# Hybrid attention layer on one core: probabilities transposed through HBM and VectorE instead of TensorE, x loaded a second time for the residual

## The chip, the cores and the metric

One core of a Trainium2 chip runs the whole program. Its engines are TensorE (PE in the profile; PEld is its weight load), VectorE (DVE), ScalarE (ACT), GpSimd (POOL) and SyncE (SP). Each takes its instructions in the order in which they were written for it and waits at an instruction until what it needs is there. Transfers are issued from the queues of SP, ACT and POOL. The metric is the device time of one execution in microseconds, as the median of several runs.

## The reference

One decoder layer on x (256 tokens x 2048), float32. Two groups of eight heads share one input projection: A, a dilated sliding-window attention with three window/dilation pairs, and B, a latent attention with low-rank q and kv. Each head's probabilities are a softmax over the keys that a query may see, and they multiply V. Then comes the output projection, a residual with RMSNorm, and a feed-forward part with squared ReLU.

```python
h = _rmsnorm(x, norm_attn_pre)
a_q, a_k, a_v, c_q, c_kv, k_r = split(h @ w_in)
# A: rotary on 32 of 128 channels, windows (128,1), (512,4), (2048,16), merged by softmax denominators
# B: q = rms(c_q) @ w_uq, [k | v] = rms(c_kv) @ w_ukv, one rotary key shared by the heads
s = einsum('bqhd,bkhd->bhqk', q, k) * scale;  s = where(key <= query, s, -1e30)
o = einsum('bhqk,bkhd->bqhd', softmax(s), v)
x = x + _rmsnorm(concat(A, B) @ w_out, norm_attn_post)
u = square(relu(_rmsnorm(x, norm_mlp_pre) @ w_up))
x = x + _rmsnorm(u @ w_down, norm_mlp_post)
```

## The kernel before

Tokens stand in two blocks of 128 (b = 0, 1), in an order in which 32x32 blocks and a rearranged trip through HBM give a full transpose: token 32 q + t of a block stands at place 4 t + q. Weights arrive as float32 tiles of 128 x 1024 on SP's queue (`raw`, five buffers), and each is split into a high part by ScalarE and a low part by VectorE (`hi`, `lo`, eight buffers each, lines 310 to 319); a product is then three TensorE passes (hi hi, hi lo, lo hi) of 512 columns. `Weights.get` keeps the splitting six tiles ahead of TensorE's place.

The order of all work is written out by a planner, `Flow` (lines 135 to 173). It has a clock that only TensorE's products move (0.2158 for one of 512 columns), and chains, which are Python generators: each emits some instructions and then yields the time after which its next part is due. `pump`, called after each group of products, lets the due chains emit. So the delays in the tables `DA`, `DB`, `D_PAIR` and others settle where in each engine's row an instruction stands; `flow.finish` and `flow.until` run chains until a condition holds, whatever their delays.

The stages: x @ w_in for A in two halves of four heads, ([q|k], v) and (q, k, v); then c_kv with the rotary key, then c_q; B's projections k0, qr, q0, v0, k1, q1, v1 (four heads in each); the output projection; and the feed-forward part, which takes two thirds of the time.

- `prelude` (lines 564 to 580) loads x by rows, in eight pieces of 256 KB into two tiles `x0`, `x1` that stay in SBUF until the residual, and afterwards squares them on ScalarE. Their sum gives `rstd_pre` (a power on GpSimd), by which the evacuations of q, k and v scale. `tables` (582 to 604) makes the rotary table `trig` on VectorE and by a Sin on ScalarE.
- `evac_a` (673 to 700): q and k of A leave PSUM on ScalarE, are rotated on VectorE, and are transposed per head: written to HBM on GpSimd's queue with rearranged rows, loaded back, and turned in 32x32 blocks by VectorE (line 698).
- `softmax_pv` (620 to 655), for every head: VectorE adds the mask and takes the maximum (626), ScalarE takes exponentials with their sums (637), VectorE normalizes (640, 642), TensorE transposes the three 128x128 blocks of probabilities that are not masked out into a PSUM bank (646), ScalarE copies them to `pT` (648), TensorE multiplies with V (653, 654), and `split` writes the head's rows of `mixT`.
- `heads_a` and `heads_b` (658 to 671, 827 to 843) run heads as workers of the planner: two workers with two heads each for a half of A, three workers for B's eight heads. Scores `sc` and outputs `o` take the PSUM banks 6 and 7 in turn (`at_bank`).
- `powers` and `residual` (895 to 952) scale x by a power of two and add the normalized output projection to it. `out_evac` uses the gains `g_post`, loaded on SP when the first block of the output projection is done (line 977), together with the release of the attention's pool `pb`.

## Time and profile before

| | us |
|---|---|
| median of 3 runs | 1031.03 (1030.07 to 1031.07) |
| profiled execution | 1030.5 |
| its span, first to last instruction | 1028.7 |
| TensorE busy | 1017.2 |
| VectorE busy | 832.2 |
| ScalarE busy | 631.3 |
| GpSimd busy | 73.4 |

The granted clock of TensorE was 0.998 over the span. In rows of the profile, a group stands as: line, engine, operation, out<-in, shapes, count, then its busy time in us and the mean ns of one, then the idle time before it and what ended it. In a timeline a row begins with the start and the length in us. Products overlap in TensorE's pipeline, so the distance between starts, not the length of one, is what a product costs its queue. The 256 tokens' attention lies between about 65 and 290 us; the output projection ends at about 343 us.

### The profile page before, as it was taken

To read this page: it belongs to the slowest core of one execution; us is meant where nothing else is said; L and a number is where in the kernel's file an instruction comes from. 1 tells how busy PE (TensorE), PEld (TensorE's weight loads), DVE (VectorE), ACT (ScalarE), POOL (GpSimd) and SP (SyncE) were. 2 spreads that over 40 slices of the span, in tenths; PEclk is the share of its full clock that TensorE was granted. 3 is DMA by queue.
4 is the path that set the end of the run, shared out by engine and by line. 5 is a ranking of instruction groups with operands and counts; after the bars stand their busy time and mean duration, and the time that the engine had idled before them with its cause. 6 is when DMAs were issued, how large, how long until landed. Compare 5 with 4: busy or idle time off the path is not lost.

```text
span 1028.7 us, 13299 instructions
## 1 busy us (share of the span) xinstructions
PE 1017.2 (99%) x4726; PEld 848.3 (82%) x4726; DVE 832.2 (81%) x1109; ACT 631.3 (61%) x838; POOL 73.4 (7%) x116
## 2 busy tenths in 40 slices
PE   9999999999999999999999999999999999999996
PEld 6888889888888888888888888888888888888885
DVE  6677647574656669998989999898999999899796
ACT  6575536565545567666775767566666665757571
POOL 0020000000001000000000100000110000211100
PEclk9999999999999999999999999999999999999999
DMA  9978457552466387777989878679979877888972
GB/s 294 361 251 268 154 179 239 177 177 84 144 225 204 104 336 259 266 255 244 297 256 303 269 243 275 195 263 340 351 268 378 287 251 255 301 313 300 317 253 82
DMA packets 106035, 257.65 MB, mean 250 GB/s; under 512 B 8944, under 2 KB 27888, under 8 KB 105584
## 3 DMA queue, kind: packets, MB, share of 16 engines
q1 hardware_dynamic: 65200, 175.14, 50.9%
q0 software_dynamic: 17392, 61.87, 18.0%
q10 hardware_dynamic: 23376, 19.78, 6.1%
q8 instruction: 37, 0.61, 0.2%
q14 instruction: 30, 0.25, 0.1%
HBM read 226.88 MB, written 29.89 MB: 250 GB/s over the span
## 4 chain that ended last, share of the span: by engine, by line
PE 85%; DMA 6%; DVE 4%; ACT 2%; issue 2%; POOL 0%; SPq 0%; DVEq 0%; POOLq 0%; ACTq 0%
PE acc_u L303 26%; PE y L303 23%; PE acc_o L303 8%; PE m L303 6%; PE md L303 5%; DMA raw<-in_w_in 4%; PE acc_k L303 3%; PE acc_v L303 3%; PE acc_ckv L303 2%; PE acc_cq L303 2%; PE acc_q L303 2%; DVE lo L314 2%; DMA ab_down<-in_w_down 1%; ACT hi L313 1%; PE sc_b L303 1%
## 5 line engine op out<-in xcount | busy, mean ns | idle before, releaser
L314 DVE TENSOR_TENSOR lo<-raw,hi 128x1024 fp32r<-128x1024 f32 (+2 forms) x205 | 232.8, 1158 | 82.8 <-ACT hi L313 81.5
L313 ACT ACTIVATE hi<-raw 128x1024 fp32r<-128x1024 f32 (+2 forms) x205 | 202.2, 1005 | 80.9 <-DMA raw<-in_w_in 23.0
L303 PE MATMUL acc_u<-hi,hT_lo 128*128 128x512 f32 x386 | 150.5, 390 | 0.4 <-DVE hT_lo L314 0.4
L303 PE MATMUL acc_u<-hi,hT_hi 128*128 128x512 f32 x386 | 150.9, 391 | 0.0
L303 PE MATMUL acc_u<-lo,hT_hi 128*128 128x512 f32 x386 | 150.3, 389 | 0.0
L303 PE MATMUL y<-lo,uhi 128*128 128x512 f32 x358 | 139.6, 390 | 0.2
L303 PE MATMUL y<-hi,uhi 128*128 128x512 f32 x358 | 139.4, 389 | 0.0
L303 PE MATMUL y<-hi,ulo 128*128 128x512 f32 x358 | 139.4, 389 | 0.0
L317 ACT ACTIVATE hi<-raw,gcol 128x1024 fp32r<-128x1024 f32 x86 | 97.1, 1149 | 36.3 <-DMA raw<-in_w_up 15.8
L318 DVE SCALAR_TENSOR_TENSOR lo<-raw,gcol,hi 128x1024 fp32r<-128x1024 f32 x86 | 106.9, 1275 | 9.6 <-ACT hi L317 9.3
L303 PEld LDWEIGHTS acc_u<-hi,hT_lo 128*128 128x128 f32 x386 | 72.5, 188 | 15.8 <-DVE hT_lo L314 0.8
L303 PEld LDWEIGHTS acc_u<-lo,hT_hi 128*128 128x128 f32 x386 | 72.5, 188 | 14.9
L303 PEld LDWEIGHTS acc_u<-hi,hT_hi 128*128 128x128 f32 x386 | 72.5, 188 | 14.9
L303 PEld LDWEIGHTS y<-lo,uhi 128*128 128x128 f32 x358 | 67.2, 188 | 14.9 <-DVE lo L314 1.1
L303 PEld LDWEIGHTS y<-hi,ulo 128*128 128x128 f32 x358 | 67.2, 188 | 14.0
L303 PEld LDWEIGHTS y<-hi,uhi 128*128 128x128 f32 x358 | 67.2, 188 | 13.9
L314 DVE TENSOR_TENSOR lo<-st_down,hi 128x1024 fp32r<-128x1024 f32 x46 | 55.0, 1219 | 0.6 <-ACT hi L313 0.6
L313 ACT ACTIVATE hi<-u 128x1024 fp32r<-128x1024 f32 (+1 forms) x33 | 32.2, 979 | 30.2 <-PE y L303 11.5
L303 PE MATMUL acc_o<-hi,mixT_hi 128*128 128x512 f32 x128 | 50.5, 395 | 0.0
L313 ACT ACTIVATE hi<-st_down 128x1024 fp32r<-128x1024 f32 x46 | 47.7, 1048 | 3.9 <-DVE st_down L370 2.5
L303 PE MATMUL md<-hi,s 128*128 128x512 f32 x138 | 50.0, 389 | 0.0
L303 PE MATMUL acc_o<-hi,mixT_lo 128*128 128x512 f32 x128 | 49.9, 390 | 0.0
(348 smaller groups left out, 2029.8 us busy)
## 6 DMA issues: line engine op xcount, KB each, us to landing
raw<-in_w_up SPq DMA_DIRECT2D x86, 512.0 KB, 4.8
raw<-in_w_down SPq DMA_DIRECT2D x82, 512.0 KB, 6.1
raw<-in_w_in SPq DMA_DIRECT2D x55, 512.0 KB, 5.3
ab<-in_w_up POOLq DMA_DIRECT2D x17, 1024.0 KB, 7.0
raw<-in_w_out SPq DMA_DIRECT2D x32, 512.0 KB, 4.8
ab_down<-in_w_down POOLq DMA_DIRECT2D x11, 1024.0 KB, 8.9
ulo<-ukeep POOLq DMA_DIRECT2D x20, 512.0 KB, 6.4
rkeep<-r ACTq DMA_DIRECT2D x28, 256.0 KB, 3.5
```

The costliest lines, as they stand in the source:

```text
L303: nc.tensor.matmul(out, a, b, start=start, stop=stop)
L313: nc.scalar.activation(hi, src, AF.Copy)
L314: nc.vector.tensor_tensor(out=lo, in0=src, in1=hi.bitcast(F32), op=OP.subtract)
L317: nc.scalar.activation(hi, src, AF.Copy, scale=g)
L318: nc.vector.scalar_tensor_tensor(out=lo, in0=src, scalar=g, in1=hi.bitcast(F32), op0=OP.mult, op1=OP.subtract)
```

## The change

The probabilities are no longer transposed on TensorE. ScalarE writes the exponentials straight into `pT`, with the columns of the three blocks rearranged, and VectorE normalizes them there. GpSimd's queue writes `pT` to HBM in runs of 96 numbers with rearranged rows (`keep`), and loads it back into `s`; VectorE turns `s` in 32x32 blocks into `pT`. V's product and the split follow as before, the split with its columns put back in order. The three PSUM transposes and the ScalarE copy of each head are gone. The planner's delays for the new steps are `D_TRIP`. A's halves have four workers with one head each, B has six, with as many buffers of `s`, `pT` and `st`.

To make room, x is not kept: `prelude` loads it in four halves of 512 KB into the buffers that q and k of A's second half use later (two of them, so that the third half waits for the first half's square), and squares each half as it comes. Two new loads of 1 MB, behind that of `g_post` on SP, bring x back for the residual. Two pads change their size, which keeps the places of the tiles in memory.

```diff
--- before.py
+++ after.py
@@ -82,7 +82,8 @@
 
 N_WARM = 8
 B_ORDER = ("k0", "qr", "q0", "v0", "k1", "q1", "v1")
-N_WORK = 3
+N_WORK = (4, 6)
+D_TRIP = (1.0, 6.0, 8.0)
 OUT_PIECES = ((0, 0, 512), (1, 0, 512), (2, 0, 512), (3, 0, 256), (3, 256, 256))
 
 
...
@@ -552,7 +553,7 @@
     weights.after[0] = [x_first]
     weights.emit(2)
 
-    xs = [mix.tile([P, D], F32, name=f"x{b}") for b in range(NB)]
+    xs = []
     cst = mix.tile([P, 704], F32, name="cst")
     freq, bias_a, bias_b = cst[:, 0:192], cst[:, 192:448], cst[:, 448:704]
     pos_i = con.tile([P, NB], I32, name="pos_i")
@@ -561,21 +562,28 @@
     ss0h = con.tile([P, NB, 2], F32, name="ss0h")
     rstd0 = []
 
+    squared = []
+
+    def square_of(half, b, pc):
+        junk = pa.tile([P, 1024], BF16, tag="v", name=f"junk0_{b}{pc}")
+        nc.scalar.activation(junk, half, AF.Square, accum_out=ss0h[:, b, pc:pc + 1])
+        squared.append((b, pc))
+        yield 0
+
     def prelude():
         yield D_X0
         nc.scalar.dma_start(out=gcol, in_=io["gains"])
-        for pc in range(4):
-            for b in range(NB):
-                c = slice(pc * 512, (pc + 1) * 512)
-                nc.sync.dma_start(out=xs[b][:, c], in_=io["x"][b * P:(b + 1) * P, c])
-                yield D_X
-        yield D_SS
         for b in range(NB):
             for pc in range(2):
-                c = slice(pc * 1024, (pc + 1) * 1024)
-                junk = pa.tile([P, 1024], BF16, tag="v", name=f"junk0_{b}{pc}")
-                nc.scalar.activation(junk, xs[b][:, c], AF.Square, accum_out=ss0h[:, b, pc:pc + 1])
-                yield 1.5
+                half = pa.tile([P, NB + 1, 512], F32, tag="qk"[pc], name=f"xh{b}{pc}")
+                half = half.rearrange("p b n -> p (b n)")[:, :1024]
+                for i in range(2):
+                    c = slice(i * 512, (i + 1) * 512)
+                    nc.sync.dma_start(out=half[:, c], in_=io["x"][b * P:(b + 1) * P, pc * 1024 + i * 512:][:, :512])
+                    yield D_X
+                flow.start(square_of(half, b, pc), D_SS)
+        while len(squared) < 4:
+            yield 1.0
         nc.vector.reduce_sum(ss0, ss0h, axis=mybir.AxisListType.X)
         rstd0.append(rstd_of(ss0, NB, D, "pre"))
 
@@ -587,8 +595,8 @@
         yield D_TAB[1]
         pos_f = con.tile([P, NB], F32, name="pos_f")
         nc.vector.tensor_copy(pos_f, pos_i)
-        ang = pa.tile([P, 2, NB, 96], F32, tag="s", bufs=2, name="ang")
-        kk_ = pa.tile([P, 2, NB, 96], F32, tag="s", bufs=2, name="kk_")
+        ang = pa.tile([P, 2, NB, 96], F32, tag="s", bufs=N_WORK[0], name="ang")
+        kk_ = pa.tile([P, 2, NB, 96], F32, tag="s", bufs=N_WORK[0], name="kk_")
         for w in range(2):
             for b in range(NB):
                 nc.vector.tensor_scalar_mul(ang[:, w, b, :], freq[:, w * 96:(w + 1) * 96], pos_f[:, b:b + 1])
@@ -619,12 +627,16 @@
 
     def softmax_pv(wk, dl, sc, bias, scale, v, head, name, need=lambda: True):
 
-        s = wk.tile([P, 384], F32, tag="s", bufs=2 if wk is pa else N_WORK, name=f"s_{name}")
-        st = wk.tile([P, 8], F32, tag="st", bufs=3, name=f"st_{name}")
-        spans = ((0, 128, bias[:, 128:256]), (128, 384, bias))
-        for i, (a, e, m) in enumerate(spans):
+        n = N_WORK[wk is not pa]
+        s = wk.tile([P, 384], F32, tag="s", bufs=n, name=f"s_{name}")
+        pT = wk.tile([P, 384], F32, tag="pT", bufs=n, name=f"pT_{name}")
+        st = wk.tile([P, 8], F32, tag="st", bufs=n, name=f"st_{name}")
+        e = pT.rearrange("p (a k c) -> p k a c", a=4, k=3)
+        spans = ((0, 1, bias[:, 128:256]), (1, 3, bias))
+        for i, (f, l, m) in enumerate(spans):
+            c = slice(f * P, l * P)
             nc.vector.tensor_tensor_reduce(
-                out=s[:, a:e], in0=sc[:, a:e], in1=m, op0=OP.add, op1=OP.max, scale=1.0,
+                out=s[:, c], in0=sc[:, c], in1=m, op0=OP.add, op1=OP.max, scale=1.0,
                 scalar=-3e38, accum_out=st[:, i:i + 1])
         if isinstance(scale, float):
             scales = [scale] * 2
@@ -633,26 +645,30 @@
             scales = [scale[:, 0, b:b + 1] for b in range(NB)]
             nc.vector.tensor_tensor(out=st[:, 2:4], in0=st[:, 0:2], in1=scale[:, 1, :], op=OP.mult)
         yield dl[2]
-        for i, (a, e, m) in enumerate(spans):
-            nc.scalar.activation(s[:, a:e], s[:, a:e], AF.Exp, bias=st[:, 2 + i:3 + i], scale=scales[i],
-                                 accum_out=st[:, 4 + i:5 + i])
+        for i, (f, l, m) in enumerate(spans):
+            nc.scalar.activation(e[:, f:l], s[:, f * P:l * P].rearrange("p (k a c) -> p k a c", a=4, c=32),
+                                 AF.Exp, bias=st[:, 2 + i:3 + i], scale=scales[i], accum_out=st[:, 4 + i:5 + i])
         yield dl[3]
         nc.vector.reciprocal(st[:, 6:8], st[:, 4:6])
-        for i, (a, e, m) in enumerate(spans):
-            nc.vector.tensor_scalar_mul(s[:, a:e], s[:, a:e], st[:, 6 + i:7 + i])
-        yield dl[4]
-        tp = tp_bank(f"pT_{name}")
-        for c in range(3):
-            transpose(tp[:, c * P:(c + 1) * P], s[:, c * P:(c + 1) * P])
-        pT = wk.tile([P, 384], F32, tag="pT", bufs=2 if wk is pa else N_WORK, name=f"pT_{name}")
-        nc.scalar.activation(pT, tp[:, :384], AF.Copy)
+        for i, (f, l, m) in enumerate(spans):
+            nc.vector.tensor_scalar_mul(e[:, f:l], e[:, f:l], st[:, 6 + i:7 + i])
+        yield D_TRIP[0]
+        keep = dram.tile([P, 384], F32, name=f"keep_{name}")
+        nc.gpsimd.dma_start(out=keep.rearrange("(a t) (q x) -> (t q) a x", a=4, q=4),
+                            in_=pT.rearrange("m (a x) -> m a x", a=4))
+        yield D_TRIP[1]
+        nc.gpsimd.dma_start(out=s, in_=keep)
+        yield D_TRIP[2]
+        nc.vector.transpose(pT.rearrange("p (k q t) -> p k q t", k=3, q=4),
+                            s.rearrange("p (q k c) -> p k q c", q=4, k=3))
         yield dl[5]
         while not need():
             yield 0.5
         o = at_bank(f"o_{name}")
         mm(o[:, :S], v[0], pT[:, :S], True, False, 2 * MM)
         mm(o[:, P:S], v[1], pT[:, S:384], False, True, MM)
-        split(mixT[0][:, head, :], mixT[1][:, head, :], o[:, :S])
+        hi, lo = [t[:, head, :].rearrange("p (b t q) -> p b t q", b=NB, q=4) for t in mixT]
+        split(hi, lo, o[:, :S].rearrange("p (b q t) -> p b t q", b=NB, q=4))
 
 
     def heads_a(qkv, half, hs, after, delay):
@@ -718,7 +734,7 @@
                 evacs.append(flow.start(evac_a(t, [[acc[i]] for acc in accs], nm, half)))
             flow.pump()
         flow.finish(*heads)
-        heads = [flow.start(heads_a(qkv, half, hs, evacs, d), 2.0) for hs, d in (((0, 1), 2.5), ((2, 3), 2.5 + D_PAIR))]
+        heads = [flow.start(heads_a(qkv, half, (h,), evacs, 2.5 + h * D_PAIR), 2.0) for h in range(4)]
 
 
     early.release()
...
@@ -865,7 +881,7 @@
                 nc.scalar.activation(t[:, h:h + 2, :].rearrange("p h s -> p (h s)"), acc, AF.Copy)
         made.add(what)
         if what == "q0":
-            workers = [flow.start(heads_b(range(w, HB, N_WORK)), w * D_PAIR) for w in range(N_WORK)]
+            workers = [flow.start(heads_b(range(w, HB, N_WORK[1])), w * D_PAIR) for w in range(N_WORK[1])]
 
 
     ssy = [con.tile([P, 4], F32, name=f"ssy{b}") for b in range(NB)]
@@ -977,6 +993,9 @@
                 nc.sync.dma_start(out=late["g_post"],
                                   in_=io["norm_attn_post"].partition_broadcast(P).rearrange("p o d -> p (o d)"))
                 late["yg"] = [po.tile([P, D], F32, name=f"yg{b}") for b in range(NB)]
+                for b_ in range(NB):
+                    xs.append(po.tile([P, D], F32, name=f"x{b_}"))
+                    nc.sync.dma_start(out=xs[b_], in_=io["x"][b_ * P:(b_ + 1) * P, :])
                 pw_chain = flow.start(powers())
             out_evac(n, b, acc[0])
             if n == 3:
```

In the changed file the lines up to 555 are numbered one higher, and later ones up to 19 higher.

**ScalarE's row in the opening.** Before; `hi23` to `hi26` are the high parts of weight tiles, `junk0` the squares of x, `ss0h` their sums:

```order
L313 ACTIVATE hi23_533<-raw23_531 128x1024
L577 ACTIVATE junk0_00_540,ss0h_127<-x0_121 128x1024
L604 ACT_TABLE_LOAD
L604 ACTIVATE trig_125<-ang_477 128x384
L577 ACTIVATE junk0_01_552,ss0h_127<-x0_121 128x1024
L313 ACTIVATE hi24_556<-raw24_554 128x1024
L577 ACTIVATE junk0_10_569,ss0h_127<-x1_122 128x1024
L313 ACTIVATE hi25_576<-raw25_574 128x1024
L577 ACTIVATE junk0_11_586,ss0h_127<-x1_122 128x1024
L313 ACTIVATE hi26_596<-raw26_594 128x1024
L680 ACTIVATE q_0_527<-acc_qk0_0_0_0_128,rstd_pre_605 128x512
L680 ACTIVATE q_0_527<-acc_qk0_0_1_0_130,rstd_pre_605 128x512
```

With the change:

```order
L314 ACTIVATE hi20_464<-raw20_462 128x1024
L569 ACTIVATE junk0_10_475,ss0h_125<-xh10_383 128x1024
L314 ACTIVATE hi21_495<-raw21_493 128x1024
L314 ACTIVATE hi22_519<-raw22_517 128x1024
L314 ACTIVATE hi23_541<-raw23_539 128x1024
L569 ACTIVATE junk0_11_548,ss0h_125<-xh11_442 128x1024
L696 ACTIVATE q_0_535<-acc_qk0_0_0_0_126,rstd_pre_555 128x512
L696 ACTIVATE q_0_535<-acc_qk0_0_1_0_128,rstd_pre_555 128x512
L696 ACTIVATE k_0_536<-acc_qk0_0_0_1_127,rstd_pre_555 128x512
L696 ACTIVATE k_0_536<-acc_qk0_0_1_1_129,rstd_pre_555 128x512
L612 ACT_TABLE_LOAD
L612 ACTIVATE trig_123<-ang_485 128x384
```

The squares have moved up, each behind the first split whose tile was loaded after that half of x; the evacuations of q and k stand ahead of the splits of tiles 24 to 26, and the table load and the Sin now stand behind the evacuations.

**GpSimd's row in A's first half.** Before, the trips of q and k of the second half:

```order
L695 DMA k_0_528<-keepk00_632 128x512
L695 DMA k_0_528<-keepk01_633 128x512
L691 DMA keepq10_911<-q_1_888 128x4x128
L691 DMA keepq11_912<-q_1_888 128x4x128
L695 DMA q_1_888<-keepq10_911 128x512
L695 DMA q_1_888<-keepq11_912 128x512
```

With the change, the heads' trips and those trips share the row (`keep_a` is a write of probabilities, `s_a` their load):

```order
L657 DMA keep_a00_870<-pT_a00_795 128x4x96
L657 DMA keep_a01_913<-pT_a01_827 128x4x96
L660 DMA s_a00_794<-keep_a00_870 128x384
L657 DMA keep_a02_947<-pT_a02_859 128x4x96
L707 DMA keepq10_955<-q_1_929 128x4x128
L707 DMA keepq11_956<-q_1_929 128x4x128
L660 DMA s_a01_826<-keep_a01_913 128x384
L657 DMA keep_a03_984<-pT_a03_896 128x4x96
L660 DMA s_a02_858<-keep_a02_947 128x384
L711 DMA q_1_929<-keepq10_955 128x512
L711 DMA q_1_929<-keepq11_956 128x512
L660 DMA s_a03_895<-keep_a03_984 128x384
```

A head's load stands behind the write of the next head or the next two; the loads of heads 1 to 3 also stand behind the writes of q, which wait for its rotation.

**TensorE's row in B.** Before, the products with V of the first three heads (`o_b`) and the scores of the next three (`sc_b`), which begin behind them; nine transposes `pT_b` stand seven places ahead of this piece:

```order
L303 MATMUL o_b0_2371<-pT_b0_2351,vB_1882 128x256
L303 MATMUL o_b0_2371<-pT_b0_2351,vB_1882 128x128
L303 MATMUL o_b1_2376<-pT_b1_2357,vB_1882 128x256
L303 MATMUL o_b1_2376<-pT_b1_2357,vB_1882 128x128
L303 MATMUL o_b2_2381<-pT_b2_2363,vB_1882 128x256
L303 MATMUL o_b2_2381<-pT_b2_2363,vB_1882 128x128
L303 MATMUL sc_b3_2386<-kT_1879,qT_1880 128x128
L303 MATMUL sc_b3_2386<-krT_1874,qrT_1881 128x128
L303 MATMUL sc_b3_2386<-kT_1879,qT_1880 128x256
L303 MATMUL sc_b3_2386<-krT_1874,qrT_1881 128x256
L303 MATMUL sc_b4_2391<-kT_1879,qT_1880 128x128
L303 MATMUL sc_b4_2391<-krT_1874,qrT_1881 128x128
```

With the change:

```order
L304 MATMUL o_b2_2523<-pT_b2_2222,vB_1876 128x256
L304 MATMUL o_b2_2523<-pT_b2_2222,vB_1876 128x128
L304 MATMUL sc_b6_2528<-kT_1873,qT_1874 128x128
L304 MATMUL sc_b6_2528<-krT_1868,qrT_1875 128x128
L304 MATMUL sc_b6_2528<-kT_1873,qT_1874 128x256
L304 MATMUL sc_b6_2528<-krT_1868,qrT_1875 128x256
L304 MATMUL o_b3_2533<-pT_b3_2247,vB_1876 128x256
L304 MATMUL o_b3_2533<-pT_b3_2247,vB_1876 128x128
L304 MATMUL sc_b7_2538<-kT_1873,qT_1874 128x128
L304 MATMUL sc_b7_2538<-krT_1868,qrT_1875 128x128
L304 MATMUL sc_b7_2538<-kT_1873,qT_1874 128x256
L304 MATMUL sc_b7_2538<-krT_1868,qrT_1875 128x256
```

With the change no transposes of probabilities are in the row, and `o_b3` stands between the scores of heads 6 and 7, which take the two banks in turn with the outputs.

4 lines of the change are left out of this document (2 added, 2 removed).

## The prediction

> **What bounds the kernel now.** I read the page's busy times first, then the table by stage, then the groups and the timeline of TensorE in the attention stages.
>
> ```profile
> span 1028.7 us, 13299 instructions
> PE 1017.2 (99%) x4726; PEld 848.3 (82%) x4726; DVE 832.2 (81%) x1109; ACT 631.3 (61%) x838; POOL 73.4 (7%) x116
> ...
> 100.00:130.00 30.00, 30.00 (x145) 25.03 (x145) 19.85 (x41) 14.30 (x27) 4.07 (x6) 1.00 0.55 170
> 220.00:250.00 30.00, 29.07 (x198) 26.75 (x197) 16.89 (x49) 15.18 (x30) 0.00 (x0) 1.00 0.38 124
> 250.00:290.00 40.00, 39.59 (x191) 32.92 (x190) 21.43 (x45) 22.79 (x44) 0.00 (x0) 1.00 0.46 142
> 290.00:340.00 50.00, 50.00 (x223) 41.41 (x221) 29.96 (x37) 24.15 (x38) 3.89 (x6) 1.00 0.66 213
> ```
>
> The stage rows give the busy time of TensorE, weight load, VectorE, ScalarE and GpSimd, then the granted clock, the DMA share and GB/s. TensorE (PE) works 1017.2 of 1028.7 us at clock 1.00, and in the attention stages, where the change is made, it idles 0.93 us (220 to 250) and 0.41 us (250 to 290). So an instruction taken off TensorE is worth its full slot, and a new wait of TensorE costs its full length. VectorE has 10 of 30 us free at 100 to 130 and 18.6 of 40 at 250 to 290.
>
> **What is removed.** 48 transposes on TensorE, three for each of 16 heads, and 16 copies of their result on ScalarE.
>
> ```profile
> L307 PE MATMUL pT_a<-ident,s_a 128*128 128x128 f32 x24 | 3.9, 272 | 0.0
> L307 PE MATMUL pT_b<-ident,s_b 128*128 128x128 f32 x24 | 3.7, 280 | 0.8 <-ACT pT_b L648 0.6
> ...
> 100.74 0.39 PE L303 MATMUL acc_k<-lo,xT_hi 128*128 128x512 f32 x1
> 100.97 0.40 PE L303 MATMUL acc_k<-hi,xT_lo 128*128 128x512 f32 x1
> 101.20 0.49 PE L307 MATMUL pT_a<-ident,s_a 128*128 128x128 f32 x3
> 101.45 0.48 PE L303 MATMUL acc_k<-hi,xT_hi 128*128 128x512 f32 x1
> 101.77 0.40 PE L303 MATMUL acc_k<-lo,xT_hi 128*128 128x512 f32 x1
> ...
> 239.47 0.40 PE L303 MATMUL acc_v<-hi,mixT_lo 128*128 128x512 f32 x1
> 239.71 0.82 PE L307 MATMUL pT_b<-ident,s_b 128*128 128x128 f32 x6
> 241.18 0.55 PE L307 MATMUL pT_b<-ident,s_b 128*128 128x128 f32 x3 [0.65 <-ACT pT_b L648]
> 241.48 0.48 PE L303 MATMUL acc_v<-hi,mixT_hi 128*128 128x512 f32 x1
> 241.80 0.39 PE L303 MATMUL acc_v<-lo,mixT_hi 128*128 128x512 f32 x1
> ...
> 276.32 0.39 PE L303 MATMUL acc_o<-hi,mixT_lo 128*128 128x512 f32 x1
> 276.56 0.81 PE L307 MATMUL pT_b<-ident,s_b 128*128 128x128 f32 x6
> 277.13 0.48 PE L303 MATMUL acc_o<-hi,mixT_hi 128*128 128x512 f32 x1
> 277.44 0.40 PE L303 MATMUL acc_o<-lo,mixT_hi 128*128 128x512 f32 x1
> ```
>
> A 512-column product starts 0.23 us after the one before (100.74 to 100.97). From 100.97 to 101.77 there would be two such steps, 0.46 us; there are 0.80, so three transposes take 0.34 us of the queue. The eight heads of A stand alone like this: 8 x 0.34 = 2.7 us. B's come in three bursts of 9, 9 and 6. The first takes 2.33 - 0.46 = 1.87 us, 0.65 of it a wait for the copy out of the second of two banks; the last 1.12 - 0.46 = 0.66; the middle one, worked out alike, 1.52. Together **6.75 us off TensorE**. The 16 ScalarE copies lie beside other work and count nothing else.
>
> By the Trainium skill ("VectorE: DVE Perf Modes", rules for kernel authors) a 128x128 transpose belongs on TensorE where a PSUM result will do, and VectorE only turns 32x32 blocks; taken as a rule for the whole program it would put the gain at nothing. The rows above go the other way here, because TensorE has no idle time in these stages and VectorE has.
>
> **What is added: the trips.** Per head one write to HBM and one load on GpSimd's queue, and one VectorE block transpose. The trace has the same trip for q and k:
>
> ```profile
> L691 POOL DMA_DIRECT2D keepq<-q x4: 762/765/942, 68.0 to 100.7; - x4
> ...
> DMA to landing us min/median/max: 3.0/4.0/5.7
> ...
> L695 POOL DMA_DIRECT2D q<-keepq x4: 548/556/565, 71.2 to 105.1; - x4
> ...
> DMA to landing us min/median/max: 3.9/6.1/7.4
> ...
> L698 DVE STREAM_TRANSPOSE q<-q x4: 1054/1084/1105, 82.5 to 116.1; 128x512 f32<-128x512 f32 x4
> ```
>
> The two landing lines are the write's (L691) and the load's (L695). The transpose of 384 columns is estimated at 1084 x 384/512 = 0.81 us, 13 us for 16, inside VectorE's free time. The trip is 4.0 + 6.1 = 10.1 us at the medians, 13.1 at both maxima. The planner leaves 6 + 8 = 14 of its microseconds; it counts 0.2158 for a product that takes 0.23, so 14.9 real ones, and 2 to 3 more before the product with V. By the order, 122 rows of TensorE lie between the first score product and its o in A (about 28 us), 156 in B (about 30). I take no wait here. Bounds: 0, and above it the price that the second rival works out.
>
> The new order does add one wait in B. Score and o banks are two, taken in turn. At 244 us the row stands o0, o1, o2, then score products; now it is o0, o1, o2, score 6, o3, score 7, and score 7 needs the bank of score 6. VectorE reads that bank only after it has finished o3.
>
> ```profile
> 244.71 0.92 PE L303 MATMUL o_b<-pT_b,vB 128*128 128x256 f32 x4 [0.28 <-DVE mixT_lo L314]
> ...
> 246.08 0.42 DVE L314 TENSOR_TENSOR mixT_lo<-o_b,mixT_hi 128x256 fp32r<-128x256 f32 x1 [0.77 <-ACT mixT_hi L313]
> ...
> 246.98 0.29 DVE L626 CUSTOM_DVE_ANT_0 s_b<-sc_b,cst 128x128 f32<-128x128 f32 x1 [0.47 <-PE sc_b L303]
> ...
> 247.19 0.42 DVE L626 CUSTOM_DVE_ANT_0 s_b<-sc_b,cst 128x256 f32<-128x256 f32 x1
> ```
>
> From an o's start to the end of its low part is 246.50 - 244.71 = 1.8 us, an o occupies 0.75 of TensorE's queue, and the two reads last 247.61 - 246.98 = 0.63. So score 7 waits 1.8 + 0.63 - 0.75 = **1.7 us**; the bounds are 0 and 2.4. The wait of 0.28 for o2 stays in this burst; a second such wait in the middle burst goes with it, since heads 4, 5 and 6, 7 now come in pairs: -0.28.
>
> **What is moved: the opening.** x now comes in four halves into two buffers, so the third half waits until the first has been squared, and SP's queue of weight loads stands behind it.
>
> ```profile
> x<-in_x SPq DMA_DIRECT2D x8, 256.0 KB, 7.4
> ...
> 31.52 0.49 SPq L570 DMA_DIRECT2D x<-in_x  x1
> ...
> 34.68 1.06 ACT L313 ACTIVATE hi<-raw 128x1024 fp32r<-128x1024 f32 x1
> ...
> 42.14 1.22 DVE L314 TENSOR_TENSOR lo<-raw,hi 128x1024 fp32r<-128x1024 f32 x1 [1.66 <-ACT hi L313]
> ...
> 47.21 0.39 PE L303 MATMUL acc_qk<-lo,xT_hi 128*128 128x512 f32 x1
> ...
> 51.47 2.08 ACT L313 ACTIVATE hi<-raw 128x1024 fp32r<-128x1024 f32 x2 [0.58 <-DVE ang L594]
> ...
> 54.60 1.28 ACT L604 ACT_TABLE_LOAD   x1
> ...
> 64.75 1.26 ACT L680 ACTIVATE q<-acc_qk,rstd_pre 128x512 f32<-128x512 f32 x2 [2.36 <-POOL rstd_pre L505]
> ...
> 88.39 0.70 PE L303 MATMUL sc_a<-k,q 128*128 128x256 f32 x2 [0.23 <-DVE k L698]
> ```
>
> The third half's first load goes out at 31.52 now. After the change it waits for the square behind the split that starts at 34.68: 34.68 + 1.06 + 1.2 = 37.0, so SP stands 5.5 us. The fourth half stands likewise from about 39 to 45. The queue is deep there: its loads land 7 us after their issue, so what was issued before keeps the DMA engines busy through most of both stops; I put the bubble at 2 to 3 us. The last tile of x @ [q|k] has its low part at 43.36 and is used at 47.21: 3.9 us of lead, and the tiles after it have more. I take no wait of TensorE there.
>
> The squares come earlier, and so does all of A: the row order puts the first score product 33 rows, 7.5 us, sooner, and its chain must follow. q leaves PSUM at 64.75 today, and TensorE already waits 0.23 us for k at 88.39; shifted, q must leave at 57.25. The last square now follows the split of tile 23, which ends at 53.55; plus 2 to 2.5 us of bubble, 1.2 for the square and 1.2 for sum and power (estimates from the rows) it is about 58.2, 1 us too late. The table load and Sin, which ran before, now stand behind all four evacuations in ScalarE's row, so the rotation of q starts another 1.26 + 1.28 us and the Sin later. Against this lateness of 3.5 to 4 us stands slack: the first load of a trip is issued at 71.2 and lands 6.1 us later, 77.3, but VectorE turns its block only at 82.5, after tiles that stand ahead in its row. Most of that slack is used by the last of the four trips. I take **0.7 us** at the first score product, with bounds 0 and 4, nearer to 0 because of the 5.2 us.
>
> **What is moved: x for the residual.** Two loads of 1 MB follow the 1 MB of g_post on SP, as the last heads finish, in front of the w_out loads. That stage uses 0.66 of the DMA engines for 213 GB/s, so 2 MB take 2000/(213/0.66) = 6 us, which delays the loads behind by no more, and these run six tiles of 12 x 0.23 us ahead. The scaling of x comes behind all three. Nothing is counted; without that cover it would be 6 us.
>
> **Sum.** -6.75 - 0.28 + 1.7 + 0.7 = -4.6 us. The profiled execution took 1030.5 us (span 1028.7): 1025.9. The median of the runs, 1031.03, is 0.5 above it: **1026.4 us**.
>
> **Rivals.** *The opening gives it back (slower).* If the DMA queue runs dry as soon as SP stops, the two stops of 5.5 and 6 us reach the tiles whole, less the lead of 3.9: 7.6 us of waiting at the end of x @ [q|k]. Then 1026.4 + 7.6 - 0.7 = 1033.3, decided by whether the low part of the last [q|k] tile ends later than 47.2 us. For it: a lead of under 4 us. Against it: 7 us of loads outstanding at each stop. Half of it gives 1029.5, no change.
>
> *The trips are late.* In B four writes and four loads stand in one GpSimd queue. If each issue had to sit out one VectorE subtraction (1.22 us, at 42.14), a burst would be 8 x 1.22 = 9.8 us late, some 4 us more than the margin of about 6, in two bursts: 1026.4 + 8 = 1034. With half that delay it is inside the margin. Against it: the eight writes issued today last 0.75 to 0.94 us each with VectorE busy two thirds of the time. The Trainium skill ("SBUF — State Buffer", two separate sides) says that GpSimd cannot write descriptors while VectorE holds their shared port, which would be the cause; the spread of 0.19 us in the trace shows little of it.
>
> *Neither new wait comes.* 1026.4 - 2.4 = 1024.0. That the transposes were hidden already is excluded by the stage rows.
>
> **Chances.** The forecast with its own range 1024 to 1028.9: 0.56. No new wait, or a little better: 0.12. The opening or the trips take most of the gain (1029 to 1033): 0.19. One of them takes more: 0.13. A measurement tells 0.2%, 2.06 us, from no change, so faster is below 1028.97: 0.68; same 0.19; slower 0.13. Range 1023.0 to 1031.5.
>
> **What would show it.** TensorE's busy time falls by about 6 us with no pT products left in its row. Between 70 and 290 us its waits are one of 1 to 2 us at score 7 in B and up to 1 us at the first score of A. Waits of o for the block transposes would refute the trips' cover; waits for a low part before 60 us would refute the opening's; a gap at 300 to 320 us would refute x's. A gain above 7 us would mean that something else moved.

## The result, and the profile after

The changed kernel takes 1038.14 us (1036.99 to 1039.18), the kernel before, on the same chip, 1030.95: a ratio of 1.0071, 95% interval 1.0054 to 1.0089. The change makes the kernel **7.2 us slower**; 1026.4 was predicted. The page of the changed kernel (its lines below 555 are numbered one higher than before) begins so:

```profile
span 1037.4 us, 13278 instructions
PE 1015.7 (98%) x4678; PEld 845.6 (82%) x4678; DVE 838.4 (81%) x1125; ACT 624.7 (60%) x822; POOL 95.0 (9%) x148
```

TensorE does as much as before less the 48 transposes, in a span that is 8.7 us longer. The view of waits, kept to TensorE, gives the total, the count and the longest of each wait:

```profile
PE sc_a L304 <- DVE k L714: 4.2, 2, 2.9
PE acc_v L304 <- DVE lo L315: 2.3, 1, 2.3
PE acc_v L304 <- ACT hi L314: 1.6, 1, 1.6
PE sc_b L304 <- DVE st_b L638: 1.5, 1, 1.5
```

The last row is the wait at score 7 that was predicted. The other three lie in the opening, where the kernel before has none above 0.4 us once the first weights are there. There is no wait of an o for a block transpose: the trips of the probabilities are covered. The table by stage, in finer windows, shows a second loss there, in the granted clock (the column behind GpSimd's count):

```profile
74.00:78.00 4.00, 4.00 (x11) 3.15 (x10) 3.91 (x4) 0.38 (x2) 1.82 (x3) 0.50 0.99 301
92.00:96.00 4.00, 3.59 (x9) 2.86 (x10) 3.97 (x9) 1.39 (x4) 0.00 (x0) 0.60 0.37 92
```

The timeline of TensorE shows how the two hang together:

```profile
70.59 0.50 PE L304 MATMUL acc_v<-hi,xT_hi 128*128 128x512 f32 x1 [1.61 <-ACT hi L314]
73.42 0.80 PE L304 MATMUL acc_v<-lo,xT_hi 128*128 128x512 f32 x1 [2.33 <-DVE lo L315]
74.01 0.63 PE L304 MATMUL acc_v<-hi,xT_lo 128*128 128x512 f32 x1
74.44 0.63 PE L304 MATMUL acc_v<-hi,xT_hi 128*128 128x512 f32 x1
...
90.66 0.46 PE L304 MATMUL sc_a<-k,q 128*128 128x128 f32 x2 [2.90 <-DVE k L714]
92.41 0.86 PE L304 MATMUL sc_a<-k,q 128*128 128x256 f32 x2 [1.29 <-DVE k L714]
```

After two idle times of 1.61 and 2.33 us a product starts 0.43 us after the one before (74.01 to 74.44), where 0.23 is usual, for some 6 us (and runs at a clock of 0.50); after 2.90 and 1.29 us again, until about 96.2. ScalarE's timeline names what the last tile of v waits for:

```profile
60.58 1.04 ACT L569 ACTIVATE junk<-xh 128x1024 bf16<-128x1024 f32 x1
...
65.33 1.27 ACT L696 ACTIVATE q<-acc_qk,rstd_pre 128x512 f32<-128x512 f32 x2 [3.62 <-POOL rstd_pre L506]
...
67.77 1.28 ACT L612 ACT_TABLE_LOAD   x1
69.06 0.52 ACT L612 ACTIVATE trig<-ang 128x384 f32<-128x384 f32 x1
69.50 4.83 ACT L314 ACTIVATE hi<-raw 128x1024 fp32r<-128x1024 f32 x5
```

The last square ends at 61.6, rstd comes at 65.3, and until then and through the evacuations, the table load and the Sin no tile is split: the next high parts start at 69.50. In the kernel before four squares, the Sin and three more splits stood ahead of the same evacuation at 64.75, and four splits right behind it.

To say where the time goes, here are starts from the timelines of TensorE (us): the last product of x @ [q|k], A's first score, the transposes of the shared key (called the end of A here; they stand 17 to 22 us behind A's last o), B's first score, the first product of the up stage, the last product of all. The kernels below the second row are those of the experiments.

| kernel | end of x @ [q|k] | first score of A | end of A | first score of B | up stage | last product |
|---|---|---|---|---|---|---|
| before | 49.48 | 87.79 | 209.13 | 226.44 | 349.54 | 1020.18 |
| after | 49.55 | 90.66 | 219.43 | 236.76 | 357.13 | 1028.56 |
| x alone | 49.24 | 88.92 | 221.65 | 238.96 | 362.09 | 1032.79 |
| four buffers, opening of before | 49.45 | 87.76 | 206.70 | 224.01 | 344.39 | 1016.46 |
| four buffers, order of the change | 49.54 | 83.59 | 213.19 | 230.52 | 350.87 | 1022.10 |
| the same, scores later | 51.09 | 86.68 | 207.53 | 224.86 | 345.22 | 1015.04 |
| two buffers, Sin first, scores later | 49.69 | 93.05 | 206.33 | 223.65 | 344.02 | 1013.84 |

From the end of x @ [q|k] to the end of A the kernel before takes 159.65 us and the changed one 169.88: 10.2 lost. From B's first score to the up stage it is 123.10 and 120.37: 2.7 won, as predicted (2.6).

### The profile page after: what moved, and what is told of

Same layout as the page of the kernel before. It is cut to its first block, busy times and chain, and to the rows that moved or that the text cites. A ratio compares the mean times of both kernels' runs of the same rounds, so it can differ in the third digit from the quotient of the medians.

```text
span 1037.4 us, 13278 instructions
## 1 busy us (share of the span) xinstructions
PE 1015.7 (98%) x4678; PEld 845.6 (82%) x4678; DVE 838.4 (81%) x1125; ACT 624.7 (60%) x822; POOL 95.0 (9%) x148
## 4 chain that ended last, share of the span: by engine, by line
PE 83%; DMA 7%; DVE 4%; ACT 2%; issue 2%; SPq 0%; POOL 0%; DVEq 0%; POOLq 0%; ACTq 0%
PE acc_u L304 26%; PE y L304 22%; PE acc_o L304 8%; PE m L304 6%; PE md L304 5%; DMA raw<-in_w_in 4%; PE acc_k L304 3%; PE acc_v L304 3%; PE acc_q L304 3%; PE acc_ckv L304 2%; DVE lo L315 2%; PE acc_cq L304 2%; DMA u<-in_w_down 1%; PE sc_b L304 1%; ACT hi L314 1%
```

## The experiments

Three theories stood against each other at first. **A**: the new handling of x in the opening costs all of it. **B**: the trips do. **C**: each does its part.

**x alone.** The kernel before, with the change's prelude and its late loads of x, and with nothing of the trips (the transposes stay on TensorE):

```diff
 # before.py
-    xs = [mix.tile([P, D], F32, name=f"x{b}") for b in range(NB)]
+    xs = []
+    (square_of and prelude of the change: halves in the tiles of tags "q" and "k")
+                for b_ in range(NB):                     # ahead of powers()
+                    xs.append(po.tile([P, D], F32, name=f"x{b_}"))
+                    nc.sync.dma_start(out=xs[b_], in_=io["x"][b_ * P:(b_ + 1) * P, :])
```

> The kernel before, with its transposes on TensorE and its three working sets, but with the change's handling of x: four halves through two buffers at the start, the rows of x loaded anew for the residual. Theory A (the handling of x in the opening costs all of the loss: SyncE's stops, the evacuations of q and k and the Sin ahead of the splits, and the low clock behind the idle times): the row order of the opening is that of the changed kernel, its loss there was 13.0 us (first score product to the end of A: 10.3 us late, plus the 2.7 us that A's transposes no longer take), so 1040 to 1045 us. Rival B (the trips of the probabilities, or their queue, cost it): 1031, as before. Rival C (each takes about half): 1035 to 1037.

Measured: 1042.74 us, ratio 1.012 (1.0104 to 1.0135). Theory A holds, B and C fall: without a single trip the kernel loses 12.8 us by the end of A (172.41 against 159.65), and TensorE waits at the same places as in the changed kernel:

```profile
PE sc_a L303 <- DVE k L705: 5.3, 2, 4.0
PE acc_v L303 <- DVE lo L314: 2.3, 1, 2.3
```

**Four buffers, opening of before.** The other half: the trips and the late loads of x stay, the opening is put back. The halves of x get four buffers from tiles that are written only later.

```diff
 # after.py
+    halves = {}
+    for b in range(NB):
+        for pc in range(2):
+            where, tag = ((pa, "qk"[pc]), (early, "e" + "qk"[pc]))[b]
+            half = where.tile([P, NB + 1, 512], F32, tag=tag, bufs=1, name=f"xh{b}{pc}")
+            halves[b, pc] = half.rearrange("p b n -> p (b n)")[:, :1024]
-    (square_of and prelude of the change)
+    (prelude of before, on halves[b, pc])
-                    t = early.tile([P, NB + 1, 512], F32, name=f"{nm}_{half}")
+                    t = early.tile([P, NB + 1, 512], F32, tag="e" + nm, bufs=1, name=f"{nm}_{half}")
```

> The changed kernel with its trips and its late loads of x for the residual, but the opening of before: x in four buffers of its own (two tiles that half 1 of A uses later, two that q and k of half 0 use later), loads and squares in the order of before. Theory A: no wait of TensorE in the opening; A's 2.7 us and B's 2.7 us (10.32 us late at B's first score, 7.59 at the first product of the up stage) stay gained, the 0.8 us lost between the first product of the up stage and the end stays lost: 1025.5 to 1026.5 us. Rival B: 1037 to 1039, as the changed kernel.

Measured: 1026.45 us, ratio 0.9966 (0.9955 to 0.9978). This is the time that was predicted for the change, 4.1 us less than the kernel before takes on the same chip (4.6 were predicted): its waits are the one at score 7 and 0.6 us at A's first score.

```profile
PE sc_b L304 <- DVE st_b L638: 1.5, 1, 1.5
...
PE sc_a L304 <- DVE k L714: 0.6, 1, 0.6
```

So the trips and the reloaded rows do what the prediction said, and the opening alone makes the change slower. The next runs ask what it is in the opening.

**Four buffers, order of the change.** Only SyncE's stops are undone; every row stands as in the changed kernel.

```diff
 # after.py
-                half = pa.tile([P, NB + 1, 512], F32, tag="qk"[pc], name=f"xh{b}{pc}")
+                half = (pa, early)[b].tile([P, NB + 1, 512], F32, tag=("", "e")[b] + "qk"[pc], bufs=1, name=f"xh{b}{pc}")
```

and the same tags for q and k of half 0.

> The changed kernel with one thing undone: the four halves of x have four buffers, so that no load of x waits for a square and SyncE never stops. The row order of all engines is that of the changed kernel: the squares early, the evacuations of q and k and the Sin ahead of the splits of the tiles behind, A's first score product 33 rows sooner than before. Theory A1 (the stops are the root; without them this order harms nothing): q leaves PSUM at about 57 us, no wait at v's last tile, at most 1 us at the first score: 1025 to 1027. Rival A2 (the row order itself costs): above 1031, with the waits of v's last tile and of the first score still there. Rival B: 1037 to 1039.

Measured: 1033.16 us, ratio 1.0028 (1.0015 to 1.0040). Neither A1 nor A2 as they were put. The waits at v's last tile are gone, so they were the stops'; the wait at the first scores is as long as ever, by the view of waits:

```profile
PE sc_a L304 <- DVE k L714: 4.2, 2, 3.1
```

The table by stage has the clock down behind it, and the DMA engines full (the last column but one) ahead of it, but nearly idle from 61 to 65 us:

```profile
61.00:65.00 4.00, 4.00 (x20) 3.30 (x19) 2.46 (x9) 3.99 (x5) 0.66 (x1) 1.00 0.01 2
70.00:80.00 10.00, 10.00 (x46) 8.29 (x45) 4.40 (x4) 5.02 (x6) 1.28 (x3) 1.00 1.04 383
80.00:90.00 10.00, 5.77 (x16) 4.13 (x15) 9.03 (x13) 5.70 (x9) 0.00 (x0) 0.69 0.75 257
```

ScalarE's timeline shows q leaving PSUM, and later the split of a tile whose raw data comes late:

```profile
58.15 1.27 ACT L696 ACTIVATE q<-acc_qk,rstd_pre 128x512 f32<-128x512 f32 x2 [4.28 <-POOL rstd_pre L506]
...
79.20 1.06 ACT L314 ACTIVATE hi<-raw 128x1024 fp32r<-128x1024 f32 x1 [1.56 <-DMA raw<-in_w_in]
```

VectorE's timeline shows what stands behind that split:

```profile
80.29 1.22 DVE L315 TENSOR_TENSOR lo<-raw,hi 128x1024 fp32r<-128x1024 f32 x1 [1.40 <-ACT hi L314]
81.43 1.09 DVE L714 STREAM_TRANSPOSE q<-q 128x512 f32<-128x512 f32 x1
```

q leaves PSUM at 58.15, as early as it was predicted to, yet the block transposes of q and k start at 81.43, one microsecond sooner than before, because VectorE has them behind the low part of a tile whose raw data lands at 79.2. That this tile lands so late has to do with the order too. In the kernel before the DMA engines work from 61 to 65 us:

```profile
61.00:65.00 4.00, 4.00 (x19) 3.30 (x19) 2.12 (x4) 1.64 (x4) 0.71 (x1) 1.00 0.93 301
```

Here, by the view of SyncE's waits up to 90 us, a weight load waits as long as 8.7 us for the low part that frees a buffer of `raw`; the longest such wait before is 5.8.

```profile
SPq L198 <- DVE lo L315: 44.4, 28, 8.7
```

No tile is split between the last square, which ends at 53.8, and the Sin, which ends at 62.4, since rstd, the evacuations and the Sin stand ahead of the splits. How much of the tile's lateness this makes no run separates. The first score product, 33 rows sooner, waits 3.06 us and the second 1.17, and the clock is down for 5 us. From the end of x @ [q|k] to the end of A: 163.65 us, 7.0 more than the 156.64 of a kernel without a wait there (below); the stops cost the other 6.2 (169.88).

**Halves on GpSimd's queue.** Two buffers, but the wait for the square stops another queue.

```diff
 # after.py
-                    nc.sync.dma_start(out=half[:, c], in_=io["x"][...])
+                    nc.gpsimd.dma_start(out=half[:, c], in_=io["x"][...])
```

> The changed kernel with one thing moved: the halves of x, still in two buffers, are loaded on GpSimd's queue, so that the wait for a square stops that queue and not the weight loads of SyncE. Theory A1 in its narrow form (what costs is that weights stand behind the stopped load): SyncE has no stop of 6 us, q leaves PSUM at 57 to 60 us, 1025 to 1028. If instead the late squares themselves cost (the third and fourth half arrive late wherever they are queued): rstd at 63 us or later and 1033 or more. GpSimd could issue late or slowly: then its rows show issues of more than 1 us.

Measured: 1030.22 us, ratio 0.9997 (0.9983 to 1.0011), no difference from before, and outside what either form expected. q leaves at 57.75, so the weights behind SyncE's stops were what held it. But TensorE loses 3 us at the very start, where it waits for high parts, and the later waits shrink by it: of 4.2 us at the first scores 1.5 are left, and the clock stays up.

```profile
PE acc_qk L304 <- ACT hi L314: 2.1, 2, 1.8
PE sc_a L304 <- DVE k L714: 1.5, 2, 1.3
```

A delay of TensorE ahead of a chain that is late anyway is free up to the lateness, and here it also saved the low clock.

**Scores later.** If the first scores only stand too early for their operands, it is enough to move them, with four buffers and everything else of the change in place.

```diff
 # four buffers, order of the change
-        heads = [flow.start(heads_a(qkv, half, (h,), evacs, 2.5 + h * D_PAIR), 2.0) for h in range(4)]
+        heads = [flow.start(heads_a(qkv, half, (h,), evacs, 2.5 + (0.0 if half else 4.0) + h * D_PAIR), 2.0) for h in range(4)]
```

> The kernel with four buffers for the halves of x (no stop of SyncE) and the row order of the changed kernel, with one thing undone: A's first score products start 4 of the planner's microseconds later, 21 rows of TensorE further down (356 instead of 335; 368 before). There TensorE waited 4.2 us for k's block transposes and then ran 5.2 us at half clock. Theory O (the scores stand too early in the row for a chain that did not get earlier by as much): these waits and the low clock behind them go, 4.2 + 2.4 us less: 1026 to 1027.5, as with the opening of before. Rival (the block transposes only move along, since they stand behind the low parts whose raw tiles come late): the wait stays, 1032 to 1033.

Measured: 1026.11 us, ratio 0.9960 (0.9946 to 0.9975). 7.0 us come back from 21 rows (4.7 us) of delay; no wait of A is left in the view. In this trace x @ [q|k] ends 1.5 us later than in the others (51.09); in that of the kernel of 1024.33 us below, which has the same opening and ends it at 48.97, the scores still wait 0.5 us.

**Sin first.** Now the stops stay, and one row order is mended.

```diff
 # after.py
-        while pre in flow.chains:
+        while pre in flow.chains or tab in flow.chains:
             yield 0.5
```

> The changed kernel, SyncE's stops and all, with one thing moved: the evacuations of q and k wait in the planner for the tables too, so that the table load and the Sin stand ahead of them and run while ScalarE waits for rstd. By the trace the splits behind start 1.8 us sooner and the rotations 3 us sooner: v's last tile waits 1.4 us instead of 1.61 + 2.33, the first low clock goes (2.6 us). TensorE then reaches the first score 5 us sooner and k's transposes come at most 3 us sooner, so that wait grows by 2 us: 1034 to 1036 in all. If the Sin's place were the whole cause: 1026 to 1028. If it does not matter: 1037 to 1039.

Measured: 1034.10 us, ratio 1.0033 (1.0018 to 1.0048), as expected: v's last tile waits no more, TensorE is early at the scores, and one wait of 6.3 us (behind it 1.0) stands there in place of four. The first score comes 2.3 us sooner (88.34), as far as the chain of q and k does, not the 3.9 us that v's waits had been.

**Two buffers, Sin first, scores later.** Both orders mended, both stops of SyncE kept.

```diff
 # after.py, with the edit "Sin first"
-        heads = [... 2.5 + h * D_PAIR ...]
+        heads = [... 2.5 + (0.0 if half else 11.0) + h * D_PAIR ...]
```

> The changed kernel with its two buffers and SyncE's two stops kept, but the order of the work changed at two places: the Sin ahead of the evacuations of q and k (as in the kernel where it stood there alone, 1034.1 us, with 6.3 + 1.0 us of wait left at the first scores) and A's first score products 11 of the planner's microseconds later (row 389 instead of 335, 12.3 us). Theory O (the stops cost only because the work that waits for them stands too early in the rows): no wait at v's last tile and none above 1 us at the first scores, no low clock after 60 us: 1025.5 to 1027.5, as with four buffers. Rival (the stops starve TensorE by themselves, wherever the scores stand): 1030 or more, with waits for high or low parts of weight tiles.

Measured: 1024.50 us, ratio 0.9946 (0.9933 to 0.9960), faster than was expected. SyncE's timeline shows the stops at their full length (31.91 to 37.49 and 40.05 to 46.01):

```profile
31.54 0.37 SPq L198 DMA_DIRECT2D raw<-in_w_in  x1
37.49 0.34 SPq L582 DMA_DIRECT2D xh<-in_x  x1
...
39.42 0.63 SPq L198 DMA_DIRECT2D raw<-in_w_in  x1
46.01 0.34 SPq L582 DMA_DIRECT2D xh<-in_x  x1
```

The view of waits, over the whole program, shows nothing in the opening above 0.3 us behind the wait for the first zeros (L527):

```profile
PE sc_b L304 <- DVE st_b L638: 1.5, 1, 1.5
PE warm L527 <- DVE zero L524: 1.2, 1, 1.2
...
PE acc_qk L304 <- ACT hi L314: 0.3, 1, 0.3
```

Once the order is mended, the stops cost nothing. So the 13.2 us that the changed kernel takes more than this one from the end of x @ [q|k] to the end of A (169.88 against 156.64) hang on the order in which the planner put the work that depends on the squares: it starts A by its own clock, and on the chip the chain behind the squares (rstd, evacuations, trips, block transposes) did not get earlier by as much.

**Empty products in the idle places.** What the low clock is worth was asked in two ways. First in the changed kernel:

```diff
 # after.py
+    def keep_busy(n):
+        for _ in range(n):
+            nc.tensor.matmul(wb, zero[:, :P], zero, start=True, stop=True)
                         for p, (x, w) in enumerate(passes):
+                            if bank_of and t == 7 and not (b or kk) and p < 2:
+                                keep_busy((8, 10)[p])
+            if nm in ("a00", "a01"):                     # ahead of the score products
+                keep_busy({"a00": 12, "a01": 5}[nm])
```

> The changed kernel with empty products (bf16 zeros into a bank that nothing reads) put into TensorE's row at the four places where it idles: 8 and 10 ahead of the first and the second product of v's last tile (1.61 and 2.33 us of idle), 12 and 5 ahead of the first and the second score (2.90 and 1.29). They fit into the idle time at about 0.22 us each. Theory K (the idle time brings the low clock, 6 and 3.5 us of it, some 4.2 us lost): the clock stays at 1.00 and the time falls by 1.6 us (the second stretch) to 4.2 us (both; part of the first is taken back by a longer wait for k): 1034 to 1036.5. If the low clock has another cause: 1038 to 1039, with the same windows at 0.5 to 0.7.

Measured: 1041.27 us, ratio 1.0098 (1.0079 to 1.0117): a miss, 3 us slower than the changed kernel instead of 2 to 4 faster. At v's waits the clock did what theory K says; at the scores it did not stay up, and the time did not fall. The table by stage:

```profile
70.00:80.00 10.00, 10.00 (x46) 6.89 (x45) 8.58 (x11) 4.94 (x6) 5.37 (x8) 1.00 0.73 233
80.00:88.00 8.00, 8.00 (x36) 5.21 (x34) 2.67 (x3) 4.33 (x5) 0.00 (x0) 1.00 1.04 389
92.00:98.00 6.00, 5.18 (x12) 4.12 (x13) 4.81 (x9) 2.15 (x6) 0.00 (x0) 0.50 0.51 156
```

and TensorE's timeline at the scores:

```profile
91.07 0.67 PE L304 MATMUL sc_a<-k,q 128*128 128x128 f32 x2 [3.06 <-DVE k L722]
92.82 1.22 PE L304 MATMUL sc_a<-k,q 128*128 128x256 f32 x2 [1.08 <-DVE k L722]
```

The clock stays at 1.00 from 70 to 88 us. TensorE then reaches the scores sooner, k comes when it comes (first score at 91.07, 90.66 without the empty products), the wait behind the empty products is again 4.1 us, and the clock is down until 97.7. So the first low clock and v's waits were not on the path at all; they lay inside the time until k was ready. The starts of the table above divide the 3 us: 0.9 are there at the end of x @ [q|k] (50.46), ahead of the empty products, 1.4 more at the end of A (221.75), with the second low clock lasting until 97.7 instead of 96.2, and 0.6 come behind the start of the up stage, where one wait for a low part lasts 1.5 us instead of 0.3. The first and the last have nothing to do with the edit, as far as the rows show.

**Pauses.** Then the cost by itself, in the kernel before, far from other waits:

```diff
 # before.py, in proj, ahead of six tiles of ckv, cq and the output projection
+    def pause(n):
+        wp_ = tp_bank(f"pause{n}")
+        nc.tensor.matmul(wp_, zero[:, :P], zero, start=True, stop=True)
+        for _ in range(n):
+            nc.gpsimd.memset(zero, 0.0)
+        nc.tensor.matmul(wp_, zero[:, :P], zero, start=True, stop=True)
```

> The kernel before, with six pauses put into TensorE's row, 15 to 30 us apart, in the projections to ckv and cq and in the output projection, where it has no other wait: an empty product, 2, 4, 6, 8, 12 or 16 memsets on GpSimd of the tile that it read, and an empty product that reads that tile again. Estimated at 0.3 to 0.4 us for a memset, the idle times are 0.8, 1.5, 2.2, 3, 4.5 and 6 us. Theory K: the short ones cost their length alone, those of 3 us and more are followed by 3 to 6 us of half clock, 0.20 us lost for each product of 0.43 instead of 0.23. Rival: every pause costs its length alone, 18 us in all, and the clock stays at 1.00.

Measured: 1077.06 us against 1030.78. The pauses came out longer than estimated, 1.23 to 10.85 us, 32.7 in all. Two of them in TensorE's timeline:

```profile
169.50 0.39 PE L470 MATMUL pause<-zero 128*128 128x512 bf16 x1 [2.45 <-POOL zero L469]
...
170.25 0.35 PE L303 MATMUL acc_ckv<-lo,xT_hi 128*128 128x288 f32 x1
170.40 0.45 PE L303 MATMUL acc_ckv<-hi,xT_lo 128*128 128x288 f32 x1
170.64 0.45 PE L303 MATMUL acc_ckv<-hi,xT_hi 128*128 128x288 f32 x1
...
325.56 0.61 PE L470 MATMUL pause<-zero 128*128 128x512 bf16 x1 [4.78 <-POOL zero L469]
...
330.23 0.63 PE L303 MATMUL acc_o<-lo,mixT_hi 128*128 128x512 f32 x1
330.66 0.46 PE L303 MATMUL acc_o<-hi,mixT_lo 128*128 128x512 f32 x1
330.95 0.40 PE L303 MATMUL acc_o<-hi,mixT_hi 128*128 128x512 f32 x1
```

The pause of 1.23 us costs its length. Behind 2.45 us the clock goes down only at 170.4, 0.9 us after the work resumed, for some 4 us. Behind 3.93, 4.78, 10.85 and 9.43 us it is down for 3.7, 5.1, 5.0 and 3.5 us, whatever the pause's length. At half clock half of these 21 us is lost, 10.6; with 32.7 of idle and twelve empty products of 0.23 that makes 46.0 of the measured 46.3. Theory K holds, with one pause of each length: the five of 2.45 us and more cost about 2 us each on top.

**A version that beats both.** The wait at score 7, the one that the change brings to B, goes when heads 6 and 7 start later. The edit was run on three kernels.

```diff
-            yield DB[0]
+            yield DB[0] + (3.0 if h >= N_WORK[1] else 0.0)
```

> The kernel with four buffers and A's first scores 21 rows later (1026.1 us), with one more edit in B: heads 6 and 7 start 3 of the planner's microseconds later, so that their score products stand 9 products (2.07 us) behind o3 instead of one ahead of it and one behind, and the bank of score 7 is free. The wait of 1.5 us at score 7 goes, one of about 0.3 us for o3's bank comes: 1.0 to 1.2 us less, 1024.9 to 1025.2. If another wait takes its place (o of heads 6 and 7 later than the output projection needs it): 1026 or more.

> The same edit in B on the kernel with four buffers and the opening of before (1026.45 us): 1.0 to 1.2 us less, 1025.2 to 1025.5; 1026.5 or more if another wait takes the place.

> The changed kernel with only its order edited at three places (no buffer added, SyncE's two stops kept): the Sin ahead of the evacuations of q and k, A's first scores 11 of the planner's microseconds later, and heads 6 and 7 of B 3 later. Theory O: the two orders of A alone gave 1024.5 us, the one of B took 1.6 us between B's first score and the first product of the up stage (120.37 to 118.74 us) on the kernels with four buffers; together 1022.5 to 1023.3 us, equal to the best kernel with four buffers (1022.97). If the stops cost something that the early orders only hid: 1024 or more.

Measured: 1024.33 us, ratio 0.9947 (0.9935 to 0.9959), with four buffers and later scores; **1022.97 us, ratio 0.9931** (0.9917 to 0.9944), with four buffers and the opening of before; 1023.90 us, ratio 0.9931 (0.9917 to 0.9946), with the change's own two buffers and only the orders mended. The ratios are to be compared, since the chips differ. From B's first score to the up stage the second takes 118.74 us (223.43 to 342.17), 1.6 less than without the edit: the wait of 1.48 is gone, and the 0.3 us expected at o3's bank is no new row, since one wait of 0.4 for a low part of o was there already. The ratio of the second falls by 0.0035, 3.6 us. The other 2 us lie, by the traces, behind the start of the up stage, where the edit changes no row (670.2 us against 672.1), so they are not the edit's. The ratios of the other two fall by 0.0013 and 0.0015, about as expected. Of the times themselves none lies in the range that was put on it: the first two are 0.6 and 2.2 us below, the third 0.6 above, and only its ratio is that of the best kernel with four buffers. With its order mended at three places the change is worth about 7 us, as much as it costs without.

## Why the prediction was wrong

- **What is removed, and the bank of score 7.** Right. A takes 159.65 us before and 156.64 where nothing waits: 3.0 won, 2.7 said. B: 2.7 won, 2.6 said; the new wait is 1.48 us, 1.7 said.
- **The trips.** Right: no wait of TensorE for them. The issues of the writes last 0.75 to 0.81 us, so nothing of the rival of late trips shows. The block transpose was priced too high, 0.81 us for 0.55 to 0.57 measured, without consequence (a nearer row is in the last section).
- **x for the residual.** Right: from 290 to 340 us TensorE is busy throughout, before and after.
- **The opening, "I take no wait of TensorE there".** True for the place that was looked at. The low part of the last tile of x @ [q|k] ends at 46.37 and is used at 47.28, so 0.9 of the 3.9 us of lead are left:

```profile
45.14 1.23 DVE L315 TENSOR_TENSOR lo<-raw,hi 128x1024 fp32r<-128x1024 f32 x1 [4.10 <-ACT hi L314]
47.28 0.39 PE L304 MATMUL acc_qk<-lo,xT_hi 128*128 128x512 f32 x1
```

  It was wrong that "the tiles after it have more": v's last tile waits 1.61 and 2.33 us. The bubble was put at 2 to 3 us once, and ScalarE idles 4.26 and 3.91 us for raw tiles, once for each stop. The last square starts at 60.58, some 5 us later than the sum had it, and the wait came at the next thing that depends on the squares, the evacuations of q and k with v's splits behind them. The rival *the opening gives it back* had the sign and a part of the cause, and the wrong place.
- **The step that failed: 0.7 us at the first score product.** It set a lateness of 3.5 to 4 us against 5.2 us of slack, and both sides were wrong. With the stops q leaves at 65.33, not at 58.2, and its rotation starts 3 us later behind that: the chain was 11 us late instead of 4. Of the 7.1 us at q, some 5 are the later square (two holes, where the sum had one smaller one) and 2 the time from the last square to q, 4.75 us where 1.2 and 1.2 were taken (the shown row at 64.75 has 2.36 us of waiting for rstd in it). That q left at 58.15 without the stops, near the 58.2, is luck: the square came earlier there, and rstd later. The slack was not there either. It had been read off the time between a landed trip and its block transpose, "after tiles that stand ahead in its row", as if these tiles would come sooner along with TensorE; they come when the DMA engines bring them, and these are full from 70 us on, after standing still while no buffer of `raw` was free. Without the stops the last transpose moved 3.1 us forward (k ends at 85.28, 88.34 before) and the score 7.5: that is the wait of 4.2 us.
- **The low clock** stands in no term. In the changed kernel it costs about 1.6 us behind the second score, in the one with four buffers 2.4, worked out from 0.43 us a product instead of 0.23. The low clock behind v's waits lies inside the time until k is ready.
- **After the up stage starts** the changed kernel loses another 0.8 us to the last product. By the table that stretch takes 670.6 us before and 671.4 after, and between 669.8 and 672.1 in kernels that have the same rows there (later scores; opening of before), so this is left unattributed.

So the opening loses 13.2 us; against it stand 3.0 us won in A and 2.7 in B, which leaves 7.5, and the 7.6 of the table. Of the 13.2, 6.2 go when the stops are undone first and the other 7.0 when the order is mended then; mended first, the order gives back all of it, with the stops still there.

## What to carry to other kernels

When a change lets a planner start something earlier, ask for every operand of it whether it comes earlier on the chip too; slack that is held by tiles waiting for DMA does not move with the consumer. A stop of a queue is paid for only where in-order work behind it blocks other work: look at the row of the engine that waits (here evacuations ahead of splits), not only at the first tile that comes late. And a wait that is filled or shortened ahead of a late chain is worth only as much as the chain itself gets sooner: 1041 with the clock kept up and the chain where it was, 1034 with v's waits gone and the chain 2.3 us sooner, 1026 and less once the scores stood where their operands are.

## What the hardware showed

TensorE's granted clock went to 0.50 behind idle time of 2.45 us in one piece, of 1.61 and 2.33 us with a single product between, and of 3.06 and 1.17 us; behind 1.23 us it stayed at 1.00. It came back after 3.5 to 5.7 us of work. The Trainium skill ("TensorE: Matmul & The Clock Gate", Part 1, what's actually happening) gives about 3.4 us of idle time for the drop and 3.4 us of sustained work for the return, by a window that runs freely. The return took as long here or up to 2.3 us longer; the drop came behind less idle time, and once 0.9 us after the idle time was over, which a free-running window would explain. No run here shows the window itself.

The block transpose of 128x384 takes 0.55 to 0.57 us here, that of 128x512 for q and k 1.09 (81.43 above), at whose rate 384 columns would take 0.82. The feed-forward part of the same kernel has a third kind:

```profile
L1046 DVE STREAM_TRANSPOSE uT<-c x16: 666/704/705, 470.3 to 602.5; 128x512 f32<-128x512 f32 x16
```

Line 1046 turns 128x512 too and reads in the same pattern as the transposes of q and k, but takes 0.70 us. By the code the two differ in what they write: line 1046 (and line 662) into consecutive columns, that of q and k into every fourth. So the writing is the likely reason; no run changes it alone. The kernel before has the same transposes in its feed-forward part at 0.70 us, which for 384 columns would have given 0.52.
